# Eight experts' two matmuls on one core: a small early store between the two halves of the last weight load

## The chip, the cores and the metric

The kernel runs on one core of one Trainium2 chip. The metric is device time in microseconds; the time before is the median of 9 runs. One more run was taken with the hardware profiler, and all views are of that run. Times in the views are counted from the first instruction of its span.

## The reference

```python
x:  [8 experts, 256 rows, 512]     float32
w1: [8 experts, 512, 2048]         float32
w2: [8 experts, 2048, 512]         float32

h = np.matmul(x, w1)
h = np.maximum(h, 0)
return np.matmul(h, w2).astype(np.float32)      # [8, 256, 512]
```

Each expert has its own two weights, and each weight is used for only 256 rows.

## The kernel before

The weights are read from HBM as float32 and written to SBUF as bf16 by the transfer itself; such a converting transfer is issued from the Pool queue (`nc.gpsimd.dma_start`). The experts are taken in four groups of two. For the first three groups one transfer brings both experts' w1 (`load_w1`) and one both experts' w2 (`load_w2`). The last group comes in smaller pieces: w1 of expert 6, w2 of expert 6, w1 of expert 7, and w2 of expert 7 in two halves of eight K blocks each, called w2_7a and w2_7b here. The list `loads` holds them in this order, and `issue(ready1, ready2)` pops from its front whatever has a buffer. There are two buffers for each weight.

x is brought in two parts: `x_head` by the SP queue as float32, cast by VectorE, and the rest by the Pool queue. TensorE transposes x (`transpose_x`), and the copies go to `xT`.

`layer1(e)` computes the hidden values of one expert: 64 matmuls of 128x256, and eight ReLU evictions by ScalarE into `hT`. `layer2(e, hT)` multiplies `hT` by w2: 32 matmuls of 128x512 into two PSUM tiles `o_ps`, one for each half of the rows. For experts 0 to 6 each half is copied by VectorE to its place in the one SBUF tile `out_sb` (L153). For expert 7 the two halves are worked in step, and are copied to a tile of their own, `out_last`, by VectorE and ScalarE. In groups of two, both experts' first layers run before their second layers; experts 6 and 7 run one after the other, so that the order at the end is second layer of 4, of 5, first and second layer of 6, first and second layer of 7.

There are two stores. `store()`, called after the second layer of expert 6, writes all of `out_sb` from the Pool queue (L89, the "big store"). After everything, the SP queue writes `out_last` (L193, the "last store").

The order on TensorE and on Pool is that of the program (`tc.manual_schedule`); waits between engines are put in by the framework from what each instruction reads and writes. Each transfer from Pool raises a semaphore by 16 when it is complete; eight semaphores are used in turn for the transfers of the Pool queue.

Of the kernel before, what the change touches and what calls it, by code (L numbers as in the profile page):

```python
# [14 lines left out]
def kernel(  # L15
# [7 lines left out]
    nc = tc.nc  # L23
    P = 128
    E, C, H = x.shape
# [13 lines left out]
    out_v = out.rearrange("e (p mo) k -> p e (mo k)", mo=MC)  # L39
# [19 lines left out]
    out_sb = const.tile([P, E - 1, MC, H], FP32, name="out_sb")  # L59
# [8 lines left out]
    def load_x():  # L68
        nc.gpsimd.dma_start(x_sb[:, HEAD * H:], x_v[:, HEAD * H:])  # L69
# [8 lines left out]
    def load_w2(es, a, b):  # L78
# [6 lines left out]
            w2_v[:, es[0]:es[-1] + 1, a * H:b * H],  # L85
        )

    def store():
        nc.gpsimd.dma_start(  # L89
            out_v[:, :E - 1, :], out_sb[:].rearrange("p e m h -> p e (m h)")  # L90
        )

    def transpose_x():


        x_r = x_sb.rearrange("p (r2 m q ko) -> p r2 m q ko", m=MC, q=P, ko=K1)
        for i, (ko, m) in enumerate((ko, m) for ko in range(K1) for m in range(MC)):
            ps = psum_t.tile([P, R // MC, P], BF16, name="xt_ps")
            for r2 in range(R // MC):
                nc.tensor.transpose(ps[:, r2, :], x_r[:, r2, m, :, ko], identity[:])  # L100
            src = ps[:].rearrange("k r2 ep -> k ep r2")
            dst = xT[:, ko, m].rearrange("k e (pp r2) -> k (e pp) r2", r2=R // MC)
            if i % 2:
                nc.scalar.copy(dst, src)  # L104
            else:
                nc.vector.tensor_copy(dst, src)  # L106

    def layer1(e):
        g = GROUP[e]
        w1_r = w1t[g][:, e - g[0], :].rearrange("p (ko q j) -> p ko q j", ko=K1, j=K2)  # L110
        hT = hT_pool.tile([P, K2, C], BF16, name="hT")
        for pr in range(K2 // 2):
            h_ps = psum_h.tile([P, 2, C], FP32, name="h_ps")
            for s in range(2):
                j = pr * 2 + s
                for ko in range(K1):
                    nc.tensor.matmul(  # L117
                        h_ps[:, s, :],
                        w1_r[:, ko, :, j],
                        xT[:, ko, :, e, :],  # L120
                        start=(ko == 0),
                        stop=(ko == K1 - 1),
                    )
            nc.scalar.activation(  # L124
                hT[:, pr * 2:pr * 2 + 2, :].rearrange("p a c -> p (a c)"),
                h_ps[:].rearrange("p a c -> p (a c)"),
                mybir.ActivationFunctionType.Relu,
            )
        return hT

    def layer2(e, hT):
        g = GROUP[e]
        last = e == E - 1
        o_ps = [psum_o.tile([P, H], FP32, name="o_ps") for _ in range(MC)]
        if last:
            order = [(k, m) for k in range(K2) for m in range(MC)]
        else:
            order = [(k, m) for m in range(MC) for k in range(K2)]
        for k, m in order:
            nc.tensor.matmul(  # L140
                o_ps[m][:],
                hT[:, k, m * P:(m + 1) * P],
                w2t[g][:, e - g[0], k * H:(k + 1) * H],
                start=(k == 0),
                stop=(k == K2 - 1),
            )
            if k == K2 - 1:
                if last and m == 1:
                    nc.scalar.copy(out_last[:, m, :], o_ps[m][:])  # L149
                elif last:  # L150
                    nc.vector.tensor_copy(out_last[:, m, :], o_ps[m][:])  # L151
                else:
                    nc.vector.tensor_copy(out_sb[:, e, m, :], o_ps[m][:])  # L153
# [3 lines left out]
    loads = []  # L157
    for i, g in enumerate(GROUPS):
        own = [(load_w1, l) for l in W1_LOADS if l[0][0] in g]
        own += [(load_w2, l) for l in W2_LOADS if l[0][0] in g]  # L160
        own.sort(key=lambda f: (f[1][0][0], f[0] is load_w2))
        loads += [(i, *f) for f in own]

    def issue(ready1, ready2):

        while loads:
            i, f, l = loads[0]
            if i >= (ready1 if f is load_w1 else ready2):
                break
            loads.pop(0)  # L170
            f(*l)
# [4 lines left out]
    with tc.manual_schedule(engines={mybir.EngineType.PE, mybir.EngineType.Pool}):  # L176
        load_x()
        make_identity(nc, identity)
        issue(B, B - 1)
        transpose_x()  # L180
        for i, g in enumerate(GROUPS):
            issue(i + B, i + B)
            whole = len(g) > 1 and (g,) in W1_LOADS
            if whole:
                hs = [layer1(e) for e in g]
                issue(i + 1 + B, i + B)
            else:
                hs = [None] * len(g)
            for e, hT in zip(g, hs):
                layer2(e, hT or layer1(e))  # L190
                if e == E - 2:
                    store()
    nc.sync.dma_start(out_v[:, E - 1, :], out_last[:].rearrange("p m h -> p (m h)"))  # L193
# [29 lines left out]
```

## Time and profile before

| | us |
|---|---|
| median of 9 runs (lowest to highest) | 181.66 (181.51 to 182.68) |
| the profiled execution | 181.63 |
| its span, first to last instruction | 179.9 |
| TensorE busy | 131.6 (73% of the span) |
| ScalarE, VectorE, Pool busy | 44.1, 16.5, 9.3 |
| Pool queue's packets, share of 16 DMA engines | 97.0% |
| TensorE's granted clock, mean | 0.899 |

HBM traffic is 71.30 MB read and 4.19 MB written. A row of a group of instructions reads: line, engine, operation, output and input, count, then busy time and mean ns of one, then the idle time of the engine just before them and what ended it. A row of the chain of waits has its start, its length and its work. In a DMA view a queue's row has packets, MB and share of the 16 engines; an issue's row has count, KB written and the median time from issue to landing. q0 is Pool's queue, q1 is SP's.

### The profile page before, as it was taken

To read this page: it belongs to the slowest core of one execution; us is meant where nothing else is said; L and a number is where in the kernel's file an instruction comes from. 1 tells how busy PE (TensorE), PEld (TensorE's weight loads), DVE (VectorE), ACT (ScalarE), POOL (GpSimd) and SP (SyncE) were. 2 spreads that over 40 slices of the span, in tenths; PEclk is the share of its full clock that TensorE was granted. 3 is DMA by queue.
4 is the path that set the end of the run, shared out by engine and by line. 5 is a ranking of instruction groups with operands and counts; after the bars stand their busy time and mean duration, and the time that the engine had idled before them with its cause. 6 is when DMAs were issued, how large, how long until landed. Compare 5 with 4: busy or idle time off the path is not lost.

```text
span 179.9 us, 1833 instructions
## 1 busy us (share of the span) xinstructions
PE 131.6 (73%) x832; PEld 92.1 (51%) x832; DVE 16.5 (9%) x20; ACT 44.1 (25%) x70; POOL 9.3 (5%) x19
## 2 busy tenths in 40 slices
PE   0017600899939994999479934999499999999950
PEld 0017500699813442899434413899334489479420
DVE  0205500000000211000003110000003110110010
ACT  2004400156600000366400000367300036026110
POOL 7000100000010001000100040000000000020000
PEclk9999965589975999699999996599969999999997
DMA  6998999999899999989999998999899899999995
GB/s 217 235 240 182 233 230 197 215 233 226 186 230 230 204 208 233 226 189 226 230 208 204 233 230 186 226 230 222 189 233 230 186 226 231 208 200 215 322 420 234
DMA packets 3703, 40.48 MB, mean 225 GB/s; under 512 B 240, under 2 KB 240, under 8 KB 1264
## 3 DMA queue, kind: packets, MB, share of 16 engines
q0 software_dynamic: 3408, 38.80, 97.0%
q1 hardware_dynamic: 288, 1.57, 2.3%
q8 instruction: 6, 0.10, 0.2%
q14 instruction: 1, 0.01, 0.0%
HBM read 71.30 MB, written 4.19 MB: 420 GB/s over the span
## 4 chain that ended last, share of the span: by engine, by line
PE 60%; DMA 27%; another core or an unknown queue 8%; POOL 1%; issue 1%; ACT 0%; POOLq 0%
PE o_ps L140 34%; DMA w_sb<-in_w_dram 27%; PE h_ps L117 26%; POOL w_sb L76 0%; POOL w_sb L69 0%; ACT out_last L149 0%; POOL identity masks.py:199 0%; POOL identity masks.py:197 0%; POOLq masks.py:199 0%; POOLq L207 0%
## 5 line engine op out<-in xcount | busy, mean ns | idle before, releaser
L117 PE MATMUL h_ps<-xT,w_sb 128*128 128x256 bf16 x512 | 64.1, 293 | 18.9 <-DMA w_sb<-in_w_dram 18.9
L117 PEld LDWEIGHTS <-w_sb 128*128 128x128 bf16 x512 | 59.8, 147 | 24.0 <-DMA w_sb<-in_w_dram 20.5
L140 PE MATMUL o_ps<-w_sb,hT 128*128 128x512 bf16 x256 | 60.7, 401 | 9.1 <-DMA w_sb<-in_w_dram 9.1
L124 ACT ACTIVATE hT<-h_ps 128x512 bf16<-128x512 f32 x64 | 38.2, 597 | 106.7 <-PE h_ps L117 106.7
L140 PEld LDWEIGHTS <-hT 128*128 128x128 bf16 x256 | 26.0, 102 | 42.3 <-issue 9.6
L153 DVE COPY out_sb<-o_ps 128x512 f32<-128x512 f32 x14 | 9.7, 692 | 128.4 <-PE o_ps L140 128.4
L100 PE MATMUL xt_ps<-identity,w_sb 128*128 128x128 bf16 x64 | 7.3, 299 | 13.9 <-DVE w_sb L175 6.7
L100 PEld LDWEIGHTS <-w_sb 128*128 128x128 bf16 x64 | 6.4, 141 | 14.7 <-DVE w_sb L175 6.7
L104 ACT COPY xT<-xt_ps 128x1024 bf16<-128x1024 bf16 x4 | 4.0, 1012 | 16.2 <-PE xt_ps L100 16.2
L83 POOL DMA_DIRECT2D w_sb<-in_w_dram x6 | 3.8, 634 | 53.2 <-PE o_ps L140 36.3
L106 DVE COPY xT<-xt_ps 128x1024 bf16<-128x1024 bf16 x4 | 4.9, 1225 | 10.4 <-PE xt_ps L100 10.4
L76 POOL DMA_DIRECT2D w_sb<-in_w_dram x5 | 3.3, 657 | 44.7 <-PE h_ps L117 44.7
L89 POOL DMA_DIRECT2D out_dram<-out_sb x1 | 1.0, 961 | 52.9 <-DVE out_sb L153 52.9
L149 ACT COPY out_last<-o_ps 128x512 f32<-128x512 f32 x1 | 0.6, 585 | 6.3 <-PE o_ps L140 6.3
L151 DVE COPY out_last<-o_ps 128x512 f32<-128x512 f32 x1 | 0.7, 692 | 13.2 <-PE o_ps L140 13.2
L175 DVE CAST w_sb<-x_head 128x2048 bf16<-128x2048 f32 x1 | 1.2, 1228 | 5.4 <-DMA x_head<-in_x_dram 5.4
L104 ACT ACT_TABLE_LOAD x1 | 1.3, 1283 | 0.7 <-PEq L207 0.7
L69 POOL DMA_DIRECT2D w_sb<-in_x_dram x1 | 0.7, 679 | 0.8 <-POOLq L207 0.8
masks.py:199 POOL TENSOR_SCALAR_AFFINE_SELECT identity<-identity 128x128 bf16<-128x128 bf16 x1 | 0.3, 287 | 0.1
masks.py:197 POOL MEMSET identity<- 128x128 bf16 x1 | 0.2, 224 | 0.0
L207 POOL MEMSET const-float32-0.0<- 128x1 f32 x1 | 0.1, 92 | 0.2 <-issue 0.2
L207 POOL MEMSET const-bfloat16-1.0<- 128x1 bf16 x1 | 0.1, 95 | 0.0
(2 smaller groups left out, 0.2 us busy)
## 6 DMA issues: line engine op xcount, KB each, us to landing
w_sb<-in_w_dram POOLq DMA_DIRECT2D x6, 4096.0 KB, 60.6
w_sb<-in_w_dram POOLq DMA_DIRECT2D x3, 2048.0 KB, 51.6
out_dram<-out_sb POOLq DMA_DIRECT2D x1, 3584.0 KB, 17.4
w_sb<-in_w_dram POOLq DMA_DIRECT2D x2, 1024.0 KB, 59.7
w_sb<-in_x_dram POOLq DMA_DIRECT2D x1, 1536.0 KB, 11.6
x_head<-in_x_dram SPq DMA_DIRECT2D x1, 1024.0 KB, 4.7
out_dram<-out_last SPq DMA_DIRECT2D x1, 512.0 KB, 4.9
```

The lines of the kernel that those rows point to most:

```text
L69: nc.gpsimd.dma_start(x_sb[:, HEAD * H:], x_v[:, HEAD * H:])
L76: nc.gpsimd.dma_start(w1t[g][:, i:i + len(es), :], w1_v[:, es[0]:es[-1] + 1, :])
L83: nc.gpsimd.dma_start(w2t[g][:, i:i + len(es), a * H:b * H], w2_v[:, es[0]:es[-1] + 1, a * H:b * H],)
L89: nc.gpsimd.dma_start(out_v[:, :E - 1, :], out_sb[:].rearrange("p e m h -> p e (m h)"))
L100: nc.tensor.transpose(ps[:, r2, :], x_r[:, r2, m, :, ko], identity[:])
L104: nc.scalar.copy(dst, src)
L106: nc.vector.tensor_copy(dst, src)
L117: nc.tensor.matmul(h_ps[:, s, :], w1_r[:, ko, :, j], xT[:, ko, :, e, :], start=(ko == 0), stop=(ko == K1 - 1),)
L124: nc.scalar.activation(hT[:, pr * 2:pr * 2 + 2, :].rearrange("p a c -> p (a c)"), h_ps[:].rearrange("p a c -> p (a c)"), mybir.ActivationF ...
L140: nc.tensor.matmul(o_ps[m][:], hT[:, k, m * P:(m + 1) * P], w2t[g][:, e - g[0], k * H:(k + 1) * H], start=(k == 0), stop=(k == K2 - 1),)
L153: nc.vector.tensor_copy(out_sb[:, e, m, :], o_ps[m][:])
L175: nc.vector.tensor_copy(x_sb[:, :HEAD * H], x_head[:])
```

## The change

The last load, w2_7b, is taken off the list. When the second layer of expert 5 has been written into the program, a new small store is issued from the Pool queue: 16 rows, experts 0, 2 and 4, the first 16 float32 values of each. Then w2_7b is put back on the list and issued. The big store is left as it was and writes all of `out_sb`, with these values among it.

```diff
+    def store_first():
+        nc.gpsimd.dma_start(
+            out_v[:16, 0:5:2, :16], out_sb[:16, 0:5:2, 0, :16]
+        )
+
     def store():
...
         loads += [(i, *f) for f in own]
+    tail = loads.pop()
...
             for e, hT in zip(g, hs):
                 layer2(e, hT or layer1(e))
+                if e == 5:
+                    issue(E, E)
+                    store_first()
+                    loads.append(tail)
+                    issue(E, E)
                 if e == E - 2:
                     store()
```

Here `out_v` is the output as [128 partitions, expert, 2 x 512], and E is 8.

In the order of the built program, Pool's last instructions change from

```
load w1 of 7; w2_7a; w2_7b; big store [waits DVE]
```

to

```
load w1 of 7; w2_7a; small store [waits DVE >= 14]; w2_7b;
big store [waits the Pool semaphores of w1 of 4 and 5 and of the small store, DVE >= 19]
```

VectorE counts its copies in the order of the program: one cast of `x_head`, four of the transposed x, then `out_sb`; count 14 is the first half of expert 4, count 19 the second half of expert 6.

## The prediction

> **What bounds the kernel now.** I read the page first: the busy shares, the DMA row of the slices, the DMA queues, and the row of the big store.
>
> ```profile
> PE 131.6 (73%) x832; PEld 92.1 (51%) x832; DVE 16.5 (9%) x20; ACT 44.1 (25%) x70; POOL 9.3 (5%) x19
> DMA  6998999999899999989999998999899899999995
> q0 software_dynamic: 3408, 38.80, 97.0%
> L89 POOL DMA_DIRECT2D out_dram<-out_sb x1 | 1.0, 961 | 52.9 <-DVE out_sb L153 52.9
> ```
>
> No engine is near its limit, but the sixteen DMA engines are: Pool's queue alone has packets on them for 97% of the span, and there is no hole from first to last slice. So the time is the bytes of one long line of transfers (x, all weights, the big store of experts 0 to 6, the last store), and only two things move the end: more work in that line, or a hole in it. The last row shows that Pool gives out the big store as soon as VectorE has copied expert 6.
>
> Next, Pool's timeline and the tail of the chain of waits.
>
> ```profile
> 105.83 0.54 POOL L76 DMA_DIRECT2D w_sb<-in_w_dram  x1
> 106.34 1.08 POOL L83 DMA_DIRECT2D w_sb<-in_w_dram  x2
> 160.37 0.96 POOL L89 DMA_DIRECT2D out_dram<-out_sb  x1 [52.95 <-DVE out_sb L153]
> ```
>
> ```profile
> 159.36 7.20 PE h_ps L117 x64
> 166.56 6.92 PE o_ps L140 x32
> 173.48 0.02 issue
> 173.50 0.58 ACT out_last L149
> ```
>
> w2_7a and w2_7b, the halves of the last expert's second weight, are issued together at 106.34 and land 57.3 and 62.1 us after their own issues by the DMA view: at 163.6 and 169.0. TensorE ends at 173.5, over 6 us before the span does. What fills those 6 us is seen in the stages at the end (columns: window, length, busy time and count of PE, PEld, DVE, ACT, POOL, then granted clock, DMA share, GB/s).
>
> ```profile
> 164.00:166.00 2.00, 2.00 (x21) 2.00 (x20) 0.00 (x0) 1.45 (x3) 0.00 (x0) 1.00 1.01 197
> 166.00:168.00 2.00, 2.00 (x14) 1.16 (x12) 0.00 (x0) 0.92 (x2) 0.00 (x0) 1.00 0.88 180
> 168.00:170.00 2.00, 2.00 (x11) 0.89 (x10) 0.00 (x0) 0.00 (x0) 0.00 (x0) 1.00 1.02 399
> 172.00:174.00 2.00, 1.47 (x7) 0.49 (x5) 0.69 (x1) 0.50 (x1) 0.00 (x0) 1.00 1.03 426
> 178.00:179.00 1.00, 0.00 (x0) 0.00 (x0) 0.00 (x0) 0.00 (x0) 0.00 (x0) 0.50 0.20 82
> 179.00:179.90 0.90, 0.00 (x0) 0.00 (x0) 0.00 (x0) 0.00 (x0) 0.00 (x0) 0.50 0.00 0
> ```
>
> Around 200 GB/s is weights (twice that is read, float32 becomes bf16); 400 and more is the store. The line changes from w2_7b to the big store between 167.4 and 168.7 without a pause and runs until 178.7. The big store was issued at 160.4, so it stood in the queue for 7 to 8 us before its turn: this is the slack that the change uses up. Last, the DMA view of 176 to 177 us.
>
> ```profile
> DMA packets 109, 0.41 MB, mean 406 GB/s; under 512 B 10, under 2 KB 10, under 8 KB 109
> q1 hardware_dynamic: 48, 0.20, 47.7%
> q0 software_dynamic: 61, 0.21, 51.2%
> ```
>
> The ten small packets are the completions of ten engines: they have finished the big store (q0) and are on the last store (q1). Six engines finish the big store only after 177.2. These six, about 1.2 us behind, set the end; they come to the big store at about 168.6, the ten others from 167.4.
>
> **The change part by part.** PE's, ACT's and DVE's instructions keep their order. On Pool the pair of w2 issues at 106.34 becomes w2_7a alone; then Pool waits for the copy of expert 4's first half (DVE count 14, the copy that ends at 135.8), issues the small store, and w2_7b directly after it. Behind the wait only those two issues are queued. In the profile's time they come at about 136.1 and 136.7. The line is then still busy with earlier loads until w2_7a lands at 163.6, so w2_7b joins 27 us before its turn and its 30 us later issue costs nothing. Without that cover each microsecond late would be a microsecond at the end.
>
> The small store itself, 48 pieces of 64 bytes, three on each engine if the 16 rows spread evenly, lies in the full line and cannot hide. The nearest rows: a weight packet of 16 KB read takes 8192 x 16 / 213 GB/s = 0.615 us on an engine, a store packet of 4 KB 4096 x 16 / 421 = 0.156 us. A line through both leaves 0.002 us without bytes, so three pieces cost 0.01 us at the low end; at the high end each costs as much as a 4 KB packet, 0.47 us. A gain from the pieces themselves is excluded, since no byte leaves the line: the big store still writes all of out_sb. I take 0.1 us, nearer to the low end, because the size is nearer to a 4-byte completion packet than to 4 KB.
>
> The Trainium skill speaks against this: "DMA: Bandwidth & Descriptors", Specifications, says that below 512 B a DMA engine does a read-modify-write. It gives no price, and no transfer of before but the completions is that small, so the trace cannot agree or disagree.
>
> The second part is a wait that the diff does not show. The small store and the big one write the same 16 rows of the output, so the big store now waits for the small one to complete (its queue's semaphore at 32; it also waits for an old load's, long done). The chain: w2_7a complete at 163.6; small store 0.1 later plus its completion; Pool's reaction 0.3 (VectorE's copy of expert 6 ends at 160.07, the issue starts at 160.37); the issue 0.96; and from its end to the first packet. For this last term the first microseconds give bounds (DMA view of 1.0 to 4.6 us).
>
> ```profile
> DMA packets 124, 1.02 MB, mean 282 GB/s; under 512 B 0, under 2 KB 0, under 8 KB 0
> q1 hardware_dynamic: 124, 1.02, 77.9%
> w_sb<-in_x_dram POOLq DMA_DIRECT2D x1, 1536.0 KB, 11.6
> x_head<-in_x_dram SPq DMA_DIRECT2D x1, 1024.0 KB, 4.7
> ```
>
> Until 4.6 no packet of Pool's queue ran, though Pool's issue of x ended at 1.93: at most 2.8 us, and the engines were busy with x_head all that time. SP's issue of x_head ended at 1.12 and its packets begin at 1.8: 0.7 us. I take 1.7, the middle. The completion: the last store's packets end at about 178.65 and it lands at 174.12 + 4.9 = 179.0, so 0.35; the most is x_head's whole fixed part, 4.7 us less 1.02 MB at about 400 GB/s (2.5), so 2.2. I take 0.5, near the low end, since that end is itself a store.
>
> Sum: 163.6 + 0.1 + 0.5 + 0.3 + 0.96 + 1.7 = 167.2, with ends at 166.0 (0.01, 0.35, 0.7) and 170.3 (0.47, 2.2, 2.8). The late engines need the big store at 168.7 now. So 1.5 us of the slack is left, and the wait costs nothing at the end; the early ten may stand still for a moment, which their 1.2 us of lead absorbs. What is late next if the chain is slower is the big store, one for one.
>
> By the same page's section on the anatomy of a Pool DMA, about 2.0 us of a transfer is fixed, most of it the write's receipt. With a completion of 2.0 the sum is 168.7, just the moment of need; the trace's only stores, at 0.35, do not show such a receipt.
>
> Two covers remain. TensorE needs w2_7b at its 17th matmul of the last expert, 166.4 + 16 x 0.216 = 169.9; it lands at 169.1 instead of 169.0. And the last store, issued at 174.1, gets its first packet at 176.1, when the ten engines are through, so 2 us of delay there is free for all but its own start-up.
>
> Total: +0.1 us. The profiled execution was 181.63 (span 179.87 and 1.77 around it), against a median of 181.66: 181.7 to 181.8, and I say 181.8. A measurement of this kernel can tell about 0.2% from no change, 0.36 us.
>
> **The rivals.**
> *The big store comes too late.* Place: Pool's new wait. It decides once the chain sums to more than 168.7, which needs 1.5 us above my values, such as a completion of 2 us while loads fill the engines (the only completion of a store in the trace ended on idle engines, which speaks for this rival). The price is the overrun: between 0 and 170.3 - 168.7 = 1.6, so 0.8 in the middle, on top of the forecast: 182.6, slower.
> *The small store stops the engines.* If the packets behind a 64-byte write wait for it, an engine loses a fixed part once, between 0.35 and 2.2 us; with the middle 1.2, 182.9. Against it: stores follow loads in one engine at 167.4 to 168.7 with no pause.
> *The later big store is a gain.* From 164 to 168 the loads move 197 and 180 GB/s where they moved 213 before: w2_7b takes 5.3 us, 1 MB at 213 would take 4.9. The waiting store may be read ahead and steal from it. If it arrives just in time, up to 0.4 to 0.5 comes back, less 0.1: 181.3. Against: it must arrive within about one microsecond.
> That the change does little of what it says is part of my forecast: what it stores early is written again.
>
> **How the numbers follow.** Forecast (hidden, +0.1) 0.41; big store late 0.30; engines stop 0.14; gain 0.15. Faster by over 0.2%: 0.15, within: 0.41, slower: 0.44. The slower cases together outweigh the forecast by a little, but no one of them does, so the predicted time is the forecast's, whose own range is 181.5 to 182.1. The range over all reaches down to 181.2 and up to 182.9: outside lie the first rival's overruns above 1.1 (a third of its 0.30), the upper half of the second's 0.14 and little of the third, about 0.2.
>
> **What would show it.** Right: the big store's issue begins at 164 to 165, blamed on a DMA; the slices near 168 us show no dip; w2_7b lands within 0.3 us of 169.0; the last packets end within 0.3 us of 178.7. Wrong: a DMA share well under 0.9 between 168 and 170 (first rival); w2_7b later by a microsecond and TensorE waiting at L140's counterpart (second); w2_7b landing before 168.8 and the end with it (third).

## The result, and the profile after

The changed kernel is faster by 0.3%: 181.32 us median of 17 runs against 181.9 us of before (now 55 runs; the nine ahead of the prediction gave 181.66), ratio 0.9968 with a 95% interval of 0.9959 to 0.9978, which is 0.4 to 0.75 us. The profiled execution took 181.16 us with a span of 179.4 us, against 181.63 and 179.9. The forecast was +0.1 us; what happened is the third rival, the gain from a later big store, which had 0.15.

Pool's timeline of the changed kernel (start, length, engine, line, what; idle time before in brackets):

```profile
108.07 0.55 POOL L83 DMA_DIRECT2D w_sb<-in_w_dram  x1
137.38 0.55 POOL L91 DMA_DIRECT2D out_dram<-out_sb  x1 [28.76 <-DVE out_sb L160]
137.92 0.57 POOL L83 DMA_DIRECT2D w_sb<-in_w_dram  x1
164.43 0.97 POOL L96 DMA_DIRECT2D out_dram<-out_sb  x1 [25.93 <-issue]
```

The order is as built: w2_7a, small store, w2_7b, big store. The big store (L96) begins 4.06 us later than before. The table of releasers names "issue" for its wait, not the DMA; that the small store's completion holds it follows from the program and from the time: the DMA view gives the small store 26.5 us from issue to landing, 137.38 + 26.5 = 163.9, 0.5 us before L96 starts.

The stages at the end (columns as in the prediction); first a row of before that the prediction does not show, for the rate ahead of the end, then the changed kernel:

```profile
160.00:162.00 2.00, 2.00 (x21) 2.00 (x19) 0.07 (x1) 1.19 (x2) 0.96 (x1) 1.00 1.02 213
```

```profile
164.00:166.00 2.00, 2.00 (x20) 2.00 (x19) 0.00 (x0) 1.31 (x3) 0.97 (x1) 1.00 1.02 213
166.00:168.00 2.00, 2.00 (x18) 1.72 (x17) 0.00 (x0) 1.45 (x3) 0.00 (x0) 1.00 0.93 256
168.00:170.00 2.00, 2.00 (x11) 0.88 (x9) 0.00 (x0) 0.23 (x1) 0.00 (x0) 1.00 1.02 418
172.00:174.00 2.00, 2.00 (x11) 0.94 (x10) 0.00 (x0) 0.00 (x0) 0.00 (x0) 1.00 1.03 424
178.00:179.00 1.00, 0.00 (x0) 0.00 (x0) 0.00 (x0) 0.00 (x0) 0.00 (x0) 0.50 0.02 8
179.00:179.39 0.39, 0.00 (x0) 0.00 (x0) 0.00 (x0) 0.00 (x0) 0.00 (x0) 0.50 0.00 0
```

From 164 to 166 the weights now move at 213 GB/s instead of 197. From 166 to 168 there are 256 instead of 180, because the change to the store comes sooner, and there is still no hole. A packet counts where it starts, and one of 8 KB is 4 GB/s in a row of 2 us, so these rates are rough. The last packets end at 178.2 instead of 178.7. TensorE ends a microsecond later than before (its second layer of expert 7 begins at 167.60, not 166.56) and that costs nothing.

The DMA view of 176 to 177 us:

```profile
DMA packets 111, 0.43 MB, mean 426 GB/s; under 512 B 7, under 2 KB 7, under 8 KB 111
q1 hardware_dynamic: 75, 0.31, 75.2%
q0 software_dynamic: 36, 0.12, 29.2%
```

Now all sixteen engines are through with the big store in this microsecond or before it. In before six of them came later than 177.2.

The gain is in w2_7b. By the traces w2_7a landed at 163.67 before and at 163.68 now; w2_7b landed 5.33 us after it before, 4.91 now; and the last store 10.00 us after that before, 9.94 now. In the trace's packet records each of w2_7b's 128 packets took 0.681 us in the mean before, and 0.625 us now; w2_7a's took 0.626 in both. The excess over 0.625, eight packets on each engine, is 0.45 us per engine before and 0.00 after. All but one of before's 39 packets of w2_7a and w2_7b that took over 0.64 us start after 165.1, and they are w2_7b's last three packets on each engine or among these. The first packet of the big store itself starts only at 167.39. In the changed kernel store packets of the early engines run from 166.88 on beside the late engines' loads, which end at 168.24, and none of these is slowed: a load does not suffer from the store packets of other engines here.

### The profile page after: what moved, and what is told of

Read it like the earlier page. It is cut to its first block, busy times and chain, and to the rows that moved or that the text cites. A ratio compares the mean times of both kernels' runs of the same rounds, so it can differ in the third digit from the quotient of the medians.

```text
span 179.4 us, 1835 instructions
## 1 busy us (share of the span) xinstructions
PE 128.0 (71%) x832; PEld 89.9 (50%) x832; DVE 16.5 (9%) x20; ACT 44.1 (25%) x70; POOL 9.9 (6%) x20
## 4 chain that ended last, share of the span: by engine, by line
PE 59%; DMA 27%; another core or an unknown queue 9%; POOL 1%; issue 1%; ACT 0%; POOLq 0%
PE o_ps L147 34%; DMA w_sb<-in_w_dram 27%; PE h_ps L124 25%; POOL w_sb L76 0%; POOL w_sb L69 0%; ACT out_last L156 0%; POOL identity masks.py:199 0%; POOL identity masks.py:197 0%; POOLq masks.py:199 0%; POOLq L220 0%
## 5 line engine op out<-in xcount | busy, mean ns | idle before, releaser
L124 PE MATMUL h_ps<-xT,w_sb 128*128 128x256 bf16 x512 | 62.0, 287 | 21.0 <-DMA w_sb<-in_w_dram 21.0
L124 PEld LDWEIGHTS <-w_sb 128*128 128x128 bf16 x512 | 58.8, 146 | 24.8 <-DMA w_sb<-in_w_dram 22.1
L107 PE MATMUL xt_ps<-identity,w_sb 128*128 128x128 bf16 x64 | 5.9, 261 | 14.2 <-DVE w_sb L183 6.7
L107 PEld LDWEIGHTS <-w_sb 128*128 128x128 bf16 x64 | 5.2, 129 | 14.9 <-DVE w_sb L183 6.7
L96 POOL DMA_DIRECT2D out_dram<-out_sb x1 | 1.0, 968 | 25.9 <-issue 25.9
L91 POOL DMA_DIRECT2D out_dram<-out_sb x1 | 0.6, 554 | 28.8 <-DVE out_sb L160 28.8
## 6 DMA issues: line engine op xcount, KB each, us to landing
out_dram<-out_sb POOLq DMA_DIRECT2D x1, 3.0 KB, 26.5
```

What stands on the lines that cost most here:

```text
L96: nc.gpsimd.dma_start(out_v[:, :E - 1, :], out_sb[:].rearrange("p e m h -> p e (m h)"))
L124: nc.tensor.matmul(h_ps[:, s, :], w1_r[:, ko, :, j], xT[:, ko, :, e, :], start=(ko == 0), stop=(ko == K1 - 1),)
```

## The experiments

Two theories. A: the new wait is the gain. A big store that already stands in the queue slows the last packets of w2_7b; issued later, it does not. B: the small store or the separate issue of w2_7b makes the gain, and the wait is harmless.

**wait_only**: no small store, w2 issues as in before, but the wait kept by other means.

```diff
...
+    def hold(k, n):
+        nc.gpsimd.tensor_copy(probe[:], w2t[GROUP[E - 1]][:, 1, k * H:k * H + 1])
+        for _ in range(n):
+            nc.gpsimd.memset(spin[:], 0.0)
...
                 if e == E - 2:
+                    hold(0, 0)
                     store()
```

> Before, with one thing added: ahead of the big store Pool copies one column of w2_7a (128x1), so that the big store is issued only after w2_7a has landed, as in the changed kernel. There is no small store, and w2_7a and w2_7b are issued together as before. Theory A (the late issue of the big store is the gain, because a store that stands in the queue slows the last packets of w2_7b): the issue starts at about 164.0, w2_7b takes 4.9 us instead of 5.3 and lands at 168.4 to 168.6, and the time is that of the changed kernel or 0.1 us better, 181.1 to 181.4, ratio to before 0.996 to 0.9975. Theory B (the small store or the separate issue of w2_7b makes the gain): w2_7b lands at 169.0, the ratio is 0.999 to 1.001.

```profile
164.00 0.19 POOL L92 COPY probe<-w_sb 128x1 bf16<-128x1 bf16 x1 [53.39 <-DMA w_sb<-in_w_dram]
164.24 0.96 POOL L97 DMA_DIRECT2D out_dram<-out_sb  x1
```

Pool's timeline shows the copy released by the load and the big store behind it, at 164.24, nearly where the changed kernel has it. Median 181.37, ratio to before 0.9958 (0.9942 to 0.9973); excess of w2_7b 0.02 us per engine, and it landed 5.00 us after w2_7a. (The profiled run itself took 181.58, with w2_7b landing at 168.95 and not by 168.6 as expected: w2_7a had landed 0.3 us later than in before. One run's time holds such shifts; the excess and the distance between the landings are free of them.) The whole gain is there without the small store. That is A.

**small_no_wait**: everything of the change but the wait. The pieces go to rows of expert 7, which only the last store writes.

```diff
-            out_v[:16, 0:5:2, :16], out_sb[:16, 0:5:2, 0, :16]
+            out_v[:16, E - 1, :].rearrange("p (a b) -> p a b", b=16)[:, 0:5:2, :], out_sb[:16, 0:5:2, 0, :16]
```

> The changed kernel with the small store's 48 pieces written into the rows of expert 7, which only the last store writes. So the big store has nothing to wait for and is issued at about 160.5 to 161.5, as in before; the small store and the late issue of w2_7b stay. Theory A: w2_7b is slowed again and lands at 169.0 to 169.2; ratio to before 1.000 to 1.002. Theory B: w2_7b lands at 168.6, and the ratio is 0.996 to 0.998 as in the changed kernel.

Pool's timeline, and the stage of 165 to 167 us in this kernel, then in the changed one, in before and in wait_only:

```profile
161.61 0.97 POOL L96 DMA_DIRECT2D out_dram<-out_sb  x1 [23.14 <-DVE out_sb L160]
```

```profile
165.00:167.00 2.00, 2.00 (x21) 2.00 (x20) 0.00 (x0) 1.45 (x3) 0.00 (x0) 1.00 1.01 176
```

```profile
165.00:167.00 2.00, 2.00 (x21) 2.00 (x19) 0.00 (x0) 1.43 (x3) 0.39 (x1) 1.00 1.03 217
```

```profile
165.00:167.00 2.00, 2.00 (x18) 1.68 (x17) 0.00 (x0) 1.45 (x3) 0.00 (x0) 1.00 1.10 193
```

```profile
165.00:167.00 2.00, 2.00 (x19) 1.83 (x18) 0.00 (x0) 1.35 (x3) 0.20 (x1) 1.00 0.98 205
```

The big store goes out as soon as VectorE is done, and the loads fall to 176 GB/s (193 in before), where the changed kernel keeps 217 (205 in wait_only). The excess is 0.45 us per engine, as in before, and w2_7b landed 5.46 us after w2_7a; median 182.11, ratio 1.0003 (0.999 to 1.0017). B falls. The run also gives the small store's own price with the separate issue: nothing beyond the interval.

**wait_longer** and **wait_w2_7b**: how late is too late.

In place of wait_only's `hold(0, 0)`; the first number chooses the K block whose column is copied (8 is the first of w2_7b), the second the number of memsets on Pool:

```diff
+                    hold(0, 6)      # wait_longer
+                    hold(8, 0)      # wait_w2_7b
```

> wait_only with six memsets of 128x128 on Pool (0.22 us each by the profile, 1.3 us or a little more in all) between the copy and the big store, so that its issue starts at about 165.5. Theory A: w2_7b stays undisturbed; the first store packet can come 2.4 us after the issue's start (in the changed kernel 164.4 to 166.9 with no pause, so at most 2.4), about 167.9: the ten early engines stand still for up to 1 us, which their lead absorbs, and the six late ones do not; ratio within 0.001 of wait_only. Theory B: ratio 1.000 or slower by the hole.

> wait_only with the copied column taken from w2_7b, so that the big store is issued after the last weights have landed, at about 168.8. All engines then stand still until its first packet, which measures the time from a Pool issue to its first packet on idle engines. Both theories: slower than before; if that time is 2.4 us, the store begins at about 171.2, 2.7 us after the late engines are free: 2.3 us slower than before, ratio 1.012; with 1.7 us ratio 1.008.

In wait_longer the big store's issue began at 165.74; median 181.44, ratio 0.9962 (0.9948 to 0.9976), excess 0.00. The first store packet came at 167.28, 1.54 us after the issue's start, just as the first engine was through with w2_7b. One and a half microseconds later cost nothing. In wait_w2_7b (Pool's timeline, then two stages):

```profile
168.84 0.19 POOL L92 COPY probe<-w_sb 128x1 bf16<-128x1 bf16 x1 [61.13 <-DMA w_sb<-in_w_dram]
169.08 0.96 POOL L97 DMA_DIRECT2D out_dram<-out_sb  x1
```

```profile
168.00:170.00 2.00, 2.00 (x11) 0.93 (x10) 0.00 (x0) 0.00 (x0) 1.11 (x2) 1.00 0.00 0
170.00:172.00 2.00, 2.00 (x11) 0.88 (x10) 0.00 (x0) 0.00 (x0) 0.04 (x1) 1.00 0.69 281
```

For two microseconds no engine moves a byte: w2_7b's last packet ends at 168.48, and the packet records have the first store packet at 170.61, 1.53 us after the issue's start, 0.57 after its end. Median 184.61, ratio 1.0127 (1.0107 to 1.0148). That is more than expected for so short a time (1.008 for 1.7 us). The late engines began the big store about 2 us later than in before; from there to the last packet it took about 0.4 us longer, and why is open. A hole like the first rival's is thus real and priced; the change stops short of it.

**issue_162_6** and **issue_163_4**: how early is too early.

The hold copies a column of w1, and then come twelve memsets or fifteen:

```diff
...
+    def hold(n):
+        nc.gpsimd.tensor_copy(probe[:], w1t[GROUP[E - 1]][:, 1, 0:1])
+        for _ in range(n):
+            nc.gpsimd.memset(spin[:], 0.0)
...
+                    hold(12)        # 15 in issue_163_4
```

> Before, with Pool held ahead of the big store by a one-column copy of expert 7's w1 (lands at about 159.1) and twelve memsets of 128x128 (0.25 us each in wait_longer), so that the big store's issue starts at about 162.4 to 162.7, between before (160.4) and wait_only (164.2). On idle engines the first packet came 1.53 us after the issue's start (wait_w2_7b). Theory A1 (the store must only be there when the last packets of w2_7b are in work, from 165.1 on in before): it is there at about 164.1, and w2_7b is slowed as in before, lands at 169.0; ratio 0.9995 to 1.001. Theory A2 (the slowing grows with the time that the store has stood in the queue): half of it, w2_7b at 168.8, ratio 0.998.

> The same with fifteen memsets: issue at about 163.2 to 163.5, store at the engines at about 164.9, just ahead of 165.1. A1: slowed as in before or nearly, w2_7b at 168.8 to 169.0, ratio 0.9985 to 1.0005. A2: a quarter of it is left, ratio 0.997.

Ratios 0.9997 (0.9986 to 1.0008) and 0.9979 (0.9966 to 0.9992): no gain at the earlier issue, some at the later. The two kernels differ by three memsets and nothing else, so this speaks for the time of the issue, though the intervals touch. The profiles do not separate A1 from A2. In that of issue_162_6 the loads ran 0.4 us late (w2_7a landed at 164.20, not 163.78), so that the two big stores were issued alike, at 163.11 and 163.00; yet the excess was 0.17 and 0.58 us, and why it differed is open. In issue_163_4 slow packets began at 164.56, when the store could just have reached the engines (163.00 + 1.53 = 164.53). In issue_162_6 the same sum gives 164.64, but slow packets begin only at 165.68. On a few late engines of these two kernels they are the fourth or fifth from the end.

**early_1_of_7**, **early_1_packet** and **early_4_packets**: how much store must stand there.

```diff
...
     def store():
-        nc.gpsimd.dma_start(
-            out_v[:, :E - 1, :], out_sb[:].rearrange("p e m h -> p e (m h)")
-        )
+        flat = out_sb[:].rearrange("p e m h -> p e (m h)")
+        nc.gpsimd.dma_start(out_v[:, 0, :], flat[:, 0, :])
+        hold(0)
+        nc.gpsimd.dma_start(out_v[:, 1:E - 1, :], flat[:, 1:, :])
```

This is early_1_of_7; `hold(0)` copies one column of w2_7a. In the last two the first transfer has rows 0 to 15 or 0 to 63 alone, one packet or four on each engine, and the other rows of expert 0 follow after the hold, in a transfer of their own.

> The big store split: expert 0 alone (eight packets of 4 KB on each engine) is issued early and stands in the queue right behind w2_7b; experts 1 to 6 are issued after w2_7a has landed, as in wait_only. Theory C (the first few store packets, read ahead, take the engine's time from the last load packets): w2_7b slowed as in before, lands at 169.0, ratio 0.9995 to 1.001. Theory D (the number of waiting store packets counts, 8 of 56): slowed by a seventh, w2_7b at 168.6, ratio 0.996 to 0.998.

> The same with only 16 rows of expert 0 issued early, one packet of 4 KB on each engine; the 112 other rows and experts 1 to 6 after w2_7a has landed, in two transfers. Theory C: one packet of 0.156 us can take about a third of the 0.46 us per engine that before lost: w2_7b at 168.7, ratio 0.997 to 0.999. Theory D: nothing to see, ratio 0.996 to 0.997.

> early_1_packet with 64 rows of expert 0 issued early, so four store packets on each engine stand behind w2_7b. One packet slowed w2_7b by 0.04 us per engine, eight by 0.51, the whole store by 0.45. If each packet read ahead takes its own 0.156 us from the loads, up to some three packets, four cost 0.4 to 0.5 (ratio 0.999 to 1.000). If the loss needs a longer line of stores than four, it is near 0.04 to 0.2 (ratio 0.996 to 0.998).

Pool's timelines of early_1_of_7 and of early_1_packet:

```profile
110.36 0.57 POOL L98 DMA_DIRECT2D out_dram<-out_sb  x1
163.87 0.19 POOL L92 COPY probe<-w_sb 128x1 bf16<-128x1 bf16 x1 [52.94 <-DMA w_sb<-in_w_dram]
164.42 0.84 POOL L100 DMA_DIRECT2D out_dram<-out_sb  x1 [0.36 <-issue]
```

```profile
109.10 0.54 POOL L98 DMA_DIRECT2D out_dram<-out_sb  x1
163.80 0.18 POOL L92 COPY probe<-w_sb 128x1 bf16<-128x1 bf16 x1 [54.15 <-DMA w_sb<-in_w_dram]
164.03 0.56 POOL L100 DMA_DIRECT2D out_dram<-out_sb  x1
```

Both have a piece of the store behind w2_7b from 110 us on and the rest after 164, and differ in the size of that piece.

| store packets per engine behind w2_7b | excess per engine, us | w2_7b landed after w2_7a, us | ratio to before |
|---|---|---|---|
| 1 | 0.04 | 5.07 | 0.998 (0.9961 to 0.9998) |
| 4 | 0.34 | 5.10 | 0.9996 (0.9983 to 1.0008) |
| 8 | 0.51 | 5.34 | 0.9993 (0.9981 to 1.0005) |
| 56 (before) | 0.45 | 5.33 | 1 |

Excess and landing are from one trace each. From eight packets on the loss does not grow with the length of the store: eight do all of it. D falls. C holds in its main point; three packets of 0.156 us make 0.47 us. One packet cost less than the 0.15 that C gave it, and four cost 0.34 where 0.4 to 0.5 was expected.

**changed_again** and **wait_only_again**, unchanged, side by side on one chip:

> The changed kernel once more, on the chip on which wait_only runs beside it. Ratio to before 0.996 to 0.9975; w2_7b undisturbed, landing 4.7 to 4.8 us after the small store. If the small store costs nothing beside the wait that it brings, it is within 0.0005 of wait_only.

> wait_only once more. Ratio to before 0.995 to 0.997. By the pieces' cost in the forecast (0.1 us) it should be 0.0005 better than the changed kernel.

Ratios 0.9973 (0.9962 to 0.9983) and 0.9975 (0.9963 to 0.9987), medians 181.47 and 181.43; excess 0.00 and 0.01. w2_7b landed 4.90 and 4.85 us after w2_7a. There is no difference to be seen. No version here beats the changed kernel; wait_only gives the same time without writing anything twice.

## Why the prediction was wrong

The step that failed is the sentence "So 1.5 us of the slack is left, and the wait costs nothing at the end". Its reasoning called the 7 to 8 us in which the big store stood in the queue slack, something that can be used up for free. It was a cost: w2_7b lost 0.45 us per engine to it, a term that the sum put at nothing. Taking the waiting away was therefore a gain, and the sign of the second part of the change was wrong: w2_7b was forecast to land at 169.1 and landed at 168.6. The stage rows shown with the prediction had the evidence (197 and 180 GB/s against 213), and the third rival read them rightly, priced it at 0.4 to 0.5 less 0.1, and gave 181.3; measured is 181.32. That the two agree so closely is luck: the rival took its 0.36 us from 181.66, and the median of before has since become 181.9. The measured gain is 0.58 us (0.4 to 0.75), more than the rival's 0.3 to 0.4; in the two traces it is 0.47, of which 0.42 is w2_7b's. The rival was held down to 0.15 by "it must arrive within about one microsecond". That condition was argued, not read from a row. The runs show a window at least 1.5 us wide, from an issue at 164.24 (wait_only) to one at 165.74 (wait_longer), with the changed kernel's 164.43 in it.

Point by point:

- What bounds the kernel, the line of transfers, was right: TensorE ended a microsecond later and the time fell.
- w2_7b's late issue costs nothing: right, it was issued 26 us before w2_7a landed.
- The small store at 0.1 us: right in size. It landed 0.17 us after w2_7a, and without the wait the ratio was 1.0003.
- The chain of the new wait: the issue was expected at 163.6 + 0.1 + 0.5 + 0.3 = 164.5 and came at 164.43. Its parts were off against each other: the completion was faster (163.9 instead of 164.2) and Pool's reaction slower (0.5 instead of 0.3).
- From the issue's end to the first packet I took 1.7 us; in wait_w2_7b, on idle engines, it is 0.57. By that the store reached the engines at about 166.0, not at 167.2, and the first rival was further off than its 0.30 said. The upper end was too wide: its 2.8 us came from engines that were at work on x_head.
- The second rival did not occur: behind the small store w2_7b's packets took 0.625 us each, with no pause.
- The write receipt of 2 us weighed from the Trainium skill ("DMA: Bandwidth & Descriptors", the section on the anatomy of a Pool DMA) is not seen here: the small store's completion came 0.17 us after that of the load ahead of it, with loads in flight, and 0.48 us after its own last packet. For the big store of wait_w2_7b, issued on idle engines, 1.53 us passed from the issue's start to the first packet and 0.52 from the last packet to the completion. Nor is a price of the same page's read-modify-write rule (Specifications) seen: the ratio of small_no_wait is 1.0003.

What stays open: that the engine reads the first store packets ahead, and that this takes its time from the loads, is the reading that fits the place (the last two or three load packets), the cap at about three store packets and the arrival in issue_163_4, but not the late start of the slow packets in issue_162_6. It was not seen directly, since the records show packets and not their reads. It also does not say why the six late engines of the changed kernel escaped: the store could have reached them at 166.0, 2.2 us before they ended w2_7b, and none of their packets was slow. The loss by the time of issue is known from a few points that scatter (0.17 and 0.58 for nearly the same time), not as a curve. And no run separates what it is about the transfer behind: the store goes the other way, in packets of 4 KB, and converts nothing; a load of the same form was not tried in its place.

## What to carry to other kernels

Where the transfers are the limit, a store that stands in the queue early need not be free: here a store behind the last load slowed that load by 0.45 us on each engine, and issuing it later, but still before the engines ran dry, gave that back. Look at the rate of the loads just ahead of the change from loads to stores, against the rate some microseconds earlier; where it sags, try the store's issue behind the landing of the last load but one. The gain is small, 0.3% here. The margin is measured from the issue: here the first packet followed 1.53 us after its start, and a store issued only after the last load cost 1.3%.

## What the runs showed of the hardware that was not expected

- Loads that waited behind loads slowed nothing (w2_7a's packets 0.626 us, with w2_7b behind it); four store packets behind w2_7b cost it 0.34 us per engine, eight 0.51, one 0.04 (one trace each).
- The 48 pieces of 64 bytes went as 16 packets of 192 bytes, 0.028 us each: the three pieces of an engine travelled together. The page's count of small packets shows them, 16 packets and 16 completions more than the 240 of before:

```profile
DMA packets 3735, 40.48 MB, mean 226 GB/s; under 512 B 272, under 2 KB 272, under 8 KB 1296
```

- On idle engines a Pool issue of 0.96 us for 3.67 MB had its first packet 0.57 us after the issue's end.
